# A fast matrix product on one core: the first two groups of rows in another order

## The chip, the cores and the metric

The kernel runs on one core of a Trainium2 chip. The metric is device time in microseconds (us) of one execution, the median over runs on the chip. Work is spread over engines that run side by side and wait for one another through semaphores: TensorE (PE; its weight loads are shown apart as PEld), VectorE (DVE), ScalarE (ACT), GpSimd (POOL), and SyncE (SP), which here issues nearly all DMAs. Each engine takes its own instructions strictly in the order in which they are written for it.

## The reference

```python
x: (8, 2048, 2048) float32, w: (2048, 2048) float32
cs = np.cumsum(x, axis=1)
diff = cs - (cs shifted by one row, zeros ahead)
return np.matmul(diff, w).astype(np.float32)
```

The difference of a running sum is `x` itself, so the kernel computes `x @ w`: 16384 rows by 2048 by 2048.

## The kernel before, in words

**Stages.** Rows come in tiles of 128. The first four tiles are multiplied plainly while `w` is loaded. All others, from tile `PLAIN` = 4 on, go in groups of four tiles: `g`, `g+1`, `h = g+2`, `h+1`. Each group is multiplied with Winograd's form of Strassen's scheme: `w` is cut into blocks B11, B12, B21, B22, the rows into A11, A12 (tile g or h) and A21, A22 (tile g+1 or h+1), and sums of blocks stand for some of the products: S1 to S4 of the rows' blocks (`total`), T1 to T4 of the blocks of `w` (`less`). The first group (`group_plain`, g = 4) uses one level of the scheme. From the second group on (`group`), several of the products are computed by a second, inner level with quarter blocks (`quarter`, `in_2` to `in_5`), whose sums of `w` are made in the first groups as well. `group` runs for g = 8, 12, 16 and so on; some of its order depends on whether g is `PLAIN + 4`, that is 8, the second group.

**Before a tile can be multiplied** it passes through a chain: `load` (SyncE: a DMA of half a tile, 512 KB, into a slot of `F`), `weigh` (ScalarE, L112: the sum of magnitudes of each row), `scale_of` (VectorE, L129 and L131, then GpSimd, L132: the row's scale `s` and its inverse `u`), `narrow` (ScalarE, L143: scaled to float16 in place), `turn` (SyncE, L156: a transposing DMA of each half into the tiles `x`). The slot of `F` is free for the next load when the tile is turned.

**Products** go into eight banks of PSUM, in pairs X, Y, Z, V. `product(to, a, b, first)` is sixteen matmuls: eight slices of the contraction, two banks. `keep` (ScalarE, L541) copies a bank, scaled, into an output tile; `add` (VectorE, L544) adds a bank to an output tile; `put` (SyncE, L555) sends it out. Output tiles `c` come from a list `free` of seven (`one_c`, `pair`) in turn, and a tile given out again waits for the DMA of its last output. In the first group, C11h is kept in a part of the tile `inner` (16 to 19) that is free until the sums of the inner level are made there. A bank can be overwritten only when the `keep` or `add` before it has read it.

**Order.** The function `after` ties every instruction to the one before it on its engine, so the order in which the helpers are called is the order on each engine. There is no scheduler to change it. What moves in the text moves past everything on the same engine, and on that engine only.

Of the kernel before, what the change touches and what calls it, by code (L numbers as in the profile page):

```python
# [10 lines left out]
def kernel(  # L11
# [30 lines left out]
    PLAIN = 4  # L42
# [78 lines left out]
    def scale_of(t):  # L121
        if t < END:
            m2 = sums_of.pop(t)
            m = small.tile([P, 1], f32, name="m1")
            s = scales[t] = small.tile([P, 1], f32, name="s")
            u = unit[t] = units.tile([P, 1], f32, name="u")
            after(
                "dve",
                lambda: nc.vector.tensor_scalar(m, m2[:, :1], m2[:, 1:], TINY, ADD, MAX),  # L129
            )  # L130
            after("dve", lambda: nc.vector.reciprocal(s, m))  # L131
            after("pool", lambda: nc.gpsimd.tensor_scalar(u, m, uw, None, MUL))  # L132
# [330 lines left out]
    def pair():  # L463
        return [one_c() for _ in range(2)]
# [34 lines left out]
    def less(dst, p, q):  # L499
        for k in range(len(dst)):  # L500
            after("dve", lambda: nc.vector.tensor_tensor(dst[k], p[k], q[k], SUB))  # L501

    def total(dst, p, q, op):
        after("dve", lambda: nc.vector.tensor_tensor(dst.all, p.all, q.all, op))  # L504
# [21 lines left out]
    def product(to, a, b, first):  # L526
        for some in steps(to, a, b, first, 4):
            some()
# [14 lines left out]
    def add(c, p, u):  # L543
        after("dve", lambda: nc.vector.scalar_tensor_tensor(c, p, u, c, MUL, ADD))  # L544

    def keeps(c, p, u):
        for n in range(2):
            keep(c[n], p[n], u)

    def adds(c, p, u):  # L550
        for n in range(2):
            add(c[n], p[n], u)
# [7 lines left out]
    def puts(c, t, h):  # L560
        for n in range(2):
            put(c[n], t, 2 * h + n)
# [26 lines left out]
    def group_plain(g, X, Y, Z, V):  # L589
        h = g + 2  # L590
        ug, uh, vg = unit[g], unit[h], unit[g + 1]
        A11g, A12g = parts(g)
        A11h, A12h = parts(h)
        A21g, A22g = parts(g + 1)
        A21h, A22h = parts(h + 1)
        S1g, S1h = S1
        S2g, S2h, S3g, S3h, S4g, S4h = A11g, A11h, A21g, A21h, A12g, A12h
        load(g + 4, 0)
        load(g + 4, 1)
        product(X, A11g, B11, True)  # L600
        for k in range(3):
            block(B22, 1, 1, k, "act")
        C11g = pair()
        keeps(C11g, X, ug)
        for k in range(3, KH):
            block(B22, 1, 1, k, "act" if k < 6 else "dve")
        product(V, A12g, B21, True)
        product(Y, A11h, B11, True)
        adds(C11g, V, ug)
        puts(C11g, g, 0)  # L610
        total(S1g, A21g, A22g, ADD)
        total(S3g, A11g, A21g, SUB)
        total(S2g, S1g, A11g, SUB)
        less(T2[:4], B22[:4], T1[:4])
        product(Z, A12h, B21, True)
        weigh(h + 1)
        C11h = [inner[:, ds(j, 2), :].rearrange("p a n -> p (a n)").bitcast(f32) for j in (16, 18)]
        keeps(C11h, Y, uh)
        scale_of(h + 1)
        narrow(h + 1)  # L620
        turn(h + 1)
        load(h + 4, 0)
        less(T2[4:], B22[4:], T1[4:])
        vh = unit[h + 1]
        product(V, S1g, T1, True)
        C22 = pair()
        keeps(C22, V, vg)
        total(S4g, A12g, S2g, SUB)
        product(X, S2g, T2, False)
        C12g = pair()  # L630
        keeps(C12g, X, ug)
        less(T3, B22, B12)
        product(V, S4g, B22, False)
        weigh(g + 4)
        scale_of(g + 4)
        narrow(g + 4)
        load(h + 4, 1)
        turn(g + 4)
        load(g + 5, 0)
        load(g + 5, 1)  # L640
        product(X, S3g, T3, False)
        total(S1h, A21h, A22h, ADD)
        total(S3h, A11h, A21h, SUB)
        total(S2h, S1h, A11h, SUB)
        adds(C11h, Z, uh)
        puts(C11h, h, 0)
        del free[-2:]
        adds(C12g, V, ug)
        puts(C12g, g, 1)
        product(Y, S2h, T2, False)  # L650
        C12h = pair()
        keeps(C12h, Y, uh)
        adds(C22, X, vg)
        puts(C22, g + 1, 1)
        total(S4h, A12h, S2h, SUB)
        product(Z, S1h, T1, True)
        weigh(h + 4)
        less(T4, B21, T2)
        scale_of(h + 4)
        C22 = pair()  # L660
        keeps(C22, Z, vh)
        narrow(h + 4)
        weigh(g + 5)
        product(Y, S3h, T3, False)
        in_2.first()
        in_2.fourth()
        load(h + 5, 0)
        load(h + 5, 1)
        scale_of(g + 5)
        adds(C22, Y, vh)  # L670
        puts(C22, h + 1, 1)
        product(Z, S4h, B22, False)
        in_2.third()
        adds(C12h, Z, uh)
        puts(C12h, h, 1)
        narrow(g + 5)
        turn(h + 4)
        product(X, A22g, T4, False)
        C21 = pair()
        keeps(C21, X, vg)  # L680
        puts(C21, g + 1, 0)
        turn(g + 5)
        load(g + 8, 0)
        load(g + 8, 1)
        product(Y, A22h, T4, False)
        weigh(h + 5)
        less(in_3.Q1, in_3.t12, in_3.t11)
        scale_of(h + 5)
        narrow(h + 5)
        less(in_3.Q2, in_3.t22, in_3.Q1)  # L690
        turn(h + 5)
        C21 = pair()
        keeps(C21, Y, vh)
        puts(C21, h + 1, 0)


    def group(g, X, Y, q, e, v, w):
# [56 lines left out]
        a11, a12, a22, s1, s2, s3, s4 = A2  # L754
        Q = in_2
        quarter(q, a11, Q.t11, True)
        add(C11g[0], q, ug)
        quarter(e, s1, Q.Q1, True)
        add(C11h[1], e, uh)
        if g == PLAIN + 4:  # L760
            total(S1g, A21g, A22g, ADD)
            total(S3g, A11g, A21g, SUB)
            total(S2g, S1g, A11g, SUB)
        quarter(v, a12, Q.t21, True)
        add(C11g[0], v, ug)
# [3 lines left out]
        quarter(e, s4, Q.t22, False)  # L769
        add(C11g[1], e, ug)  # L770
        put(C11g[1], g, 1)
        if g > PLAIN + 4:
            total(S1h, A21h, A22h, ADD)
            total(S3h, A11h, A21h, SUB)
        scale_of(next_g)
        narrow(next_g)
        if g > PLAIN + 4:
            total(S2h, S1h, A11h, SUB)
        go(P6g, 2)
        quarter(q, s3, Q.Q3, False)  # L780
        add(C11h[1], q, uh)
        put(C11h[1], h, 1)
        if g == PLAIN + 4:
            total(S1h, A21h, A22h, ADD)
            total(S3h, A11h, A21h, SUB)
            total(S2h, S1h, A11h, SUB)
        weigh(next_h)
        load(next_k, 1)
        total(S4g, A12g, S2g, SUB)
        go(P6g, 2)  # L790
        C12g = pair()
        keeps(C12g, X, ug)
        turn(next_g, [0])
        quarter(q, a22, Q.Q4, False)
        add(C11h[0], q, uh)
# [5 lines left out]
        if five:  # L801
            one()
            two()
        scale_of(next_h)
        narrow(next_h)
        load(next_l, 1)
        one, two, A3 = sums_in(
            S4g, S4h, (S2h.half(0), S2h.half(1), S4h.half(0), passing[2])
        )
# [86 lines left out]
        else:  # L896
            if g == PLAIN + 4:
                in_3.third()
            one()
            two()  # L900
            weigh(next_k)
            seven(A3, in_3, C12g, C12h, P7g)
            turn(next_g, [1])
# [108 lines left out]
```

## Time and profile before

| | us |
|---|---|
| median of 3 runs | 1492.88 (1492.49 to 1496.3) |
| the profiled execution | 1496.11 |
| its span, first to last instruction | 1494.3 |
| TensorE busy | 1473.4 (99%) |
| VectorE busy | 1283.9 (86%) |
| ScalarE busy | 913.6 (61%) |
| granted clock of TensorE | 0.999 |

Times within the profile are counted from the start of the span. A row of a timeline has the start, the time to the end of the last of the merged instructions, engine, line, operation, what is written and read, their number, and in brackets the idle time of the engine before it with what ended that. The first group's products begin near 76 us, the second group's near 127 us, the third's near 177 us, the fourth's near 223 us. A program line of a helper stands for all its uses: L501 is `less`, L504 `total`, L514 a matmul of `product`, L533 one of `quarter`, L555 `put`.

### The profile page before, as it was taken

The numbers are of one execution on the slowest core, as the hardware profiler recorded it, in microseconds if no ns is written. First come the engines' busy times: TensorE is split into PE (matmuls) and PEld (weight loads), VectorE is DVE, ScalarE is ACT, GpSimd is POOL, SyncE is SP. The second block draws the span as 40 slices with busy tenths as digits, with TensorE's granted clock in tenths as the row PEclk, the third lists the DMA queues.
The fourth block names the chain that finished last, engine by engine and source line by source line (L and its number), as shares of the span: only waits on it lengthen the run. The fifth ranks groups of instructions, "written<-read, shape, count | busy, mean of one in ns | idle before, by whom it ended". The sixth has DMA issues, their size and how long they took to land.

```text
span 1494.3 us, 21105 instructions
## 1 busy us (share of the span) xinstructions
PE 1473.4 (99%) x6793; PEld 663.4 (44%) x6799; DVE 1283.9 (86%) x2419; ACT 913.6 (61%) x1301; POOL 69.4 (5%) x136
## 2 busy tenths in 40 slices
PE   8999999999999999999999999999999999999998
PEld 3444444444444444444444444444444444444443
DVE  7997878888888888888888888888888888888887
ACT  5876565655666656666656656556657556656542
POOL 0110000000000000000000000000000000000000
PEclk9999999999999999999999999999999999999999
DMA  9999979999999999999999998999899999899973
GB/s 362 352 233 254 244 224 255 263 271 249 259 258 241 260 276 250 255 251 251 265 269 242 266 248 255 261 272 248 257 239 261 268 257 262 252 238 265 273 204 130
DMA packets 386255, 382.59 MB, mean 256 GB/s; under 512 B 275744, under 2 KB 275744, under 8 KB 386016
## 3 DMA queue, kind: packets, MB, share of 16 engines
q1 hardware_dynamic: 385584, 379.41, 92.6%
q0 software_dynamic: 560, 1.84, 0.3%
q8 instruction: 53, 0.87, 0.2%
q14 instruction: 58, 0.48, 0.1%
HBM read 180.88 MB, written 135.27 MB: 212 GB/s over the span
## 4 chain that ended last, share of the span: by engine, by line
PE 88%; DMA 5%; DVE 3%; ACT 2%; issue 1%; SPq 1%; DVEq 0%; ACTq 0%
PE b L533 45%; PE b L514 41%; DVE c L544 2%; PE b L250 2%; DMA W<-in_w_dram 2%; DMA F<-in_x_dram 2%; DMA x<-F 1%; DVE W L501 1%; ACT waste L112 0%; DMA W<-in_x_dram 0%; DMA out_dram<-wb 0%; ACT F L143 0%; SPq L156 0%; DVE x L504 0%; ACT wb L234 0%
## 5 line engine op out<-in xcount | busy, mean ns | idle before, releaser
L544 DVE SCALAR_TENSOR_TENSOR c<-b,u,c 128x512 f32<-128x512 f32 x1046 | 743.2, 746 | 161.6 <-PE b L533 91.5
L514 PE MATMUL b<-W,x 128*128 128x512 f16 x3072 | 717.4, 379 | 4.3 <-ACT c L541 3.5
L541 ACT ACTIVATE c<-b,u 128x512 f32<-128x512 f32 x494 | 315.9, 681 | 334.5 <-PE b L533 164.0
L514 PEld LDWEIGHTS <-x 128*128 128x128 f16 x3072 | 300.3, 98 | 369.1 <-issue 6.3
L143 ACT ACTIVATE F<-F,s 128x1024 f16<-128x1024 f32 x246 | 282.2, 1147 | 111.2 <-DVE s L131 107.2
L533 PE MATMUL b<-W,inner 128*128 128x512 f16 x1392 | 338.3, 379 | 0.0
L112 ACT ACTIVATE waste<-F 128x1024 uint8<-128x1024 f32 x246 | 259.6, 1055 | 107.5 <-DMA F<-in_x_dram 103.7
L533 PEld LDWEIGHTS <-inner 128*128 128x128 f16 x1744 | 170.6, 98 | 207.1 <-issue 1.6
L533 PEld LDWEIGHTS <-x 128*128 128x128 f16 x1560 | 152.4, 98 | 192.3 <-issue 12.2
L533 PE MATMUL b<-W,x 128*128 128x512 f16 x968 | 234.3, 379 | 1.7 <-DVE c L544 0.3
L504 DVE TENSOR_TENSOR x<-x,x 128x1024 f16<-128x1024 f16 (+1 forms) x214 | 120.5, 574 | 6.2 <-PE b L514 1.1
L132 POOL TENSOR_SCALAR u<-m,uw 128x1 f32<-128x1 f32 x124 | 64.4, 525 | 1311.3 <-DVE m L129 1303.3
L533 PE MATMUL b<-flow,x 128*128 128x512 f16 x352 | 90.3, 379 | 0.7 <-DVE c L544 0.7
L504 DVE TENSOR_TENSOR inner<-x,x 128x1024 f16<-128x1024 f16 (+1 forms) x122 | 67.5, 553 | 1.2 <-DMA x<-F 1.1
L533 PE MATMUL b<-inner 128*128 128x512 f16 x240 | 61.6, 379 | 1.1 <-DVE c L544 1.1
L250 PE MATMUL b<-wb,xP 128*128 128x512 bf16 x234 | 57.0, 393 | 5.4 <-ACT wb L234 3.8
L533 PE MATMUL b<-inner,x 128*128 128x512 f16 x240 | 61.6, 379 | 0.0
L112 ACT ACTIVATION_READ_ACCUMULATOR waste<-F 128x1 f32 x246 | 46.6, 190 | 0.0
L504 DVE TENSOR_TENSOR x<-inner,x 128x1024 f16<-128x1024 f16 x62 | 42.4, 684 | 3.2
L504 DVE TENSOR_TENSOR inner<-inner 128x512 f16<-128x512 f16 x112 | 42.4, 420 | 1.0
L501 DVE TENSOR_TENSOR flow<-W,inner 128x512 f16<-128x512 f16 x120 | 42.6, 416 | 0.0
L234 ACT CAST wb<-W 128x1024 bf16<-128x1024 f32 x32 | 32.2, 1059 | 15.6 <-DMA W<-in_w_dram 12.3
(56 smaller groups left out, 420.0 us busy)
## 6 DMA issues: line engine op xcount, KB each, us to landing
out_dram<-c SPq DMA_DIRECT2D x494, 256.0 KB, 4.1
F<-in_x_dram SPq DMA_DIRECT2D x246, 512.0 KB, 5.2
flow<-spill SPq DMA_DIRECT2D x57, 512.0 KB, 4.8
W<-in_w_dram SPq DMA_DIRECT2D x32, 512.0 KB, 10.0
W<-in_x_dram SPq DMA_DIRECT2D x16, 256.0 KB, 7.2
x<-F SPq DMA_TRANSPOSE x246, 4.0
out_dram<-o POOLq DMA_DIRECT2D x5, 256.0 KB, 4.1
out_dram<-o SPq DMA_DIRECT2D x5, 256.0 KB, 3.6
```

The source lines that it names most:

```text
L112: lambda: nc.scalar.activation(waste, where[t][i], ABS, scale=1.0 / ROW, accum_out=sums_of[t][:, i : i + 1],),
L132: after("pool", lambda: nc.gpsimd.tensor_scalar(u, m, uw, None, MUL))
L143: lambda: nc.scalar.activation(narrowed(t)[:, ds(i * NH, NH)], where[t][i], COPY, scale=s),
L234: after("act", lambda: nc.scalar.copy(b, wt))
L250: lambda: nc.tensor.matmul(ps[r][n], xP[:, r, ko, :], wb[h, ko][:, ds(n * NB, NB)], start=(ko == 0), stop=(ko == KO - 1),),
L501: after("dve", lambda: nc.vector.tensor_tensor(dst[k], p[k], q[k], SUB))
L504: after("dve", lambda: nc.vector.tensor_tensor(dst.all, p.all, q.all, op))
L514: said = nc.tensor.matmul(to[n], a[k], b[k][:, n, :], start=(first and k == 0), stop=(k == KH - 1), skip_group_check=True,)
L533: said = nc.tensor.matmul(to, a[k], b[k], start=(first and k == 0), stop=(k == 3), skip_group_check=True)
L541: after("act", lambda: nc.scalar.activation(c, p, COPY, scale=u))
L544: after("dve", lambda: nc.vector.scalar_tensor_tensor(c, p, u, c, MUL, ADD))
```

## The change

Nothing is added or left out; instructions are put in another order, and one pair of output tiles lies elsewhere.

In `group_plain` (first group):
- T2 = B22 - T1, eight pieces: the first goes ahead of `adds(C11g)`, the second behind it, four behind the sums of x, and two behind `scale_of(h + 1)` (before: four and four). T4 is split around `scale_of(h + 4)`.
- C22g lies in `inner` (20 to 23) rather than in two tiles `c`; its `keeps` go ahead of `narrow(h + 1)`. Likewise `keeps(C21, Y)` goes ahead of `narrow(h + 5)`.
- The transposes of h+4 and g+5 are issued one half at a time, some earlier; those of h+5 go ahead of the two loads of g+8. `weigh(h + 5)` is earlier.

In `group` with g = 8 (second group):
- S1g and S3g go between the additions of the first two quarter products; S1h, S3h and S2h ahead of `scale_of(next_g)` and its narrowing, which go behind half of the product P6g (X, S2g, T2) and one quarter product.
- `keeps(C12g)` goes ahead of `weigh(next_h)`; `scale_of(next_h)`, `narrow(next_h)` and one load go behind the product P6h (Y, S2h, T2), its keeps and the sums of x that `seven` needs.

Later groups keep their order.

```diff
@@ group_plain
         product(Y, A11h, B11, True)
+        less(T2[:1], B22[:1], T1[:1])
         adds(C11g, V, ug)
         puts(C11g, g, 0)
+        less(T2[1:2], B22[1:2], T1[1:2])
         total(S1g, A21g, A22g, ADD)
         total(S3g, A11g, A21g, SUB)
         total(S2g, S1g, A11g, SUB)
-        less(T2[:4], B22[:4], T1[:4])
+        less(T2[2:6], B22[2:6], T1[2:6])
         product(Z, A12h, B21, True)
         weigh(h + 1)
-        C11h = [inner[:, ds(j, 2), :].rearrange("p a n -> p (a n)").bitcast(f32) for j in (16, 18)]
+        C11h, C22g = (
+            [
+                inner[:, ds(j, 2), :].rearrange("p a n -> p (a n)").bitcast(f32)
+                for j in (i, i + 2)
+            ]
+            for i in (16, 20)
+        )
         keeps(C11h, Y, uh)
         scale_of(h + 1)
+        less(T2[6:], B22[6:], T1[6:])
+        vh = unit[h + 1]
+        product(V, S1g, T1, True)
+        keeps(C22g, V, vg)
         narrow(h + 1)
         turn(h + 1)
         load(h + 4, 0)
-        less(T2[4:], B22[4:], T1[4:])
-        vh = unit[h + 1]
-        product(V, S1g, T1, True)
-        C22 = pair()
-        keeps(C22, V, vg)
         total(S4g, A12g, S2g, SUB)
         product(X, S2g, T2, False)
         C12g = pair()
...
-        adds(C22, X, vg)
-        puts(C22, g + 1, 1)
+        adds(C22g, X, vg)
+        puts(C22g, g + 1, 1)
+        del free[-2:]
         total(S4h, A12h, S2h, SUB)
         product(Z, S1h, T1, True)
         weigh(h + 4)
-        less(T4, B21, T2)
+        less(T4[:4], B21[:4], T2[:4])
         scale_of(h + 4)
-        C22 = pair()
-        keeps(C22, Z, vh)
+        less(T4[4:], B21[4:], T2[4:])
+        C22h = pair()
+        keeps(C22h, Z, vh)
         narrow(h + 4)
         weigh(g + 5)
         product(Y, S3h, T3, False)
...
         load(h + 5, 0)
         load(h + 5, 1)
+        turn(h + 4, [0])
         scale_of(g + 5)
...
         narrow(g + 5)
-        turn(h + 4)
+        weigh(h + 5)
+        turn(h + 4, [1])
+        turn(g + 5, [0])
         product(X, A22g, T4, False)
         C21 = pair()
         keeps(C21, X, vg)
         puts(C21, g + 1, 0)
-        turn(g + 5)
-        load(g + 8, 0)
-        load(g + 8, 1)
+        turn(g + 5, [1])
         product(Y, A22h, T4, False)
-        weigh(h + 5)
         less(in_3.Q1, in_3.t12, in_3.t11)
         scale_of(h + 5)
+        C21 = pair()
+        keeps(C21, Y, vh)
         narrow(h + 5)
         less(in_3.Q2, in_3.t22, in_3.Q1)
         turn(h + 5)
-        C21 = pair()
-        keeps(C21, Y, vh)
+        load(g + 8, 0)
+        load(g + 8, 1)
         puts(C21, h + 1, 0)
@@ group
         quarter(q, a11, Q.t11, True)
+        if g == PLAIN + 4:
+            total(S1g, A21g, A22g, ADD)
         add(C11g[0], q, ug)
+        if g == PLAIN + 4:
+            total(S3g, A11g, A21g, SUB)
         quarter(e, s1, Q.Q1, True)
         add(C11h[1], e, uh)
         if g == PLAIN + 4:
-            total(S1g, A21g, A22g, ADD)
-            total(S3g, A11g, A21g, SUB)
             total(S2g, S1g, A11g, SUB)
...
         put(C11g[1], g, 1)
+        total(S1h, A21h, A22h, ADD)
+        total(S3h, A11h, A21h, SUB)
+        if g == PLAIN + 4:
+            total(S2h, S1h, A11h, SUB)
         if g > PLAIN + 4:
-            total(S1h, A21h, A22h, ADD)
-            total(S3h, A11h, A21h, SUB)
-        scale_of(next_g)
-        narrow(next_g)
-        if g > PLAIN + 4:
+            scale_of(next_g)
+            narrow(next_g)
             total(S2h, S1h, A11h, SUB)
         go(P6g, 2)
         quarter(q, s3, Q.Q3, False)
         add(C11h[1], q, uh)
         put(C11h[1], h, 1)
         if g == PLAIN + 4:
-            total(S1h, A21h, A22h, ADD)
-            total(S3h, A11h, A21h, SUB)
-            total(S2h, S1h, A11h, SUB)
-        weigh(next_h)
+            scale_of(next_g)
+            narrow(next_g)
+        else:
+            weigh(next_h)
         load(next_k, 1)
         total(S4g, A12g, S2g, SUB)
         go(P6g, 2)
         C12g = pair()
         keeps(C12g, X, ug)
+        if g == PLAIN + 4:
+            weigh(next_h)
         turn(next_g, [0])
...
-        scale_of(next_h)
-        narrow(next_h)
-        load(next_l, 1)
+        if g > PLAIN + 4:
+            scale_of(next_h)
+            narrow(next_h)
+            load(next_l, 1)
...
             one()
             two()
+            if g == PLAIN + 4:
+                scale_of(next_h)
+                narrow(next_h)
+                load(next_l, 1)
             weigh(next_k)
             seven(A3, in_3, C12g, C12h, P7g)
```

More of the change, by code (lines that the diff above doesn't have):

```diff
@@ L668, in group_plain @@
         load(h + 5, 1)
+        turn(h + 4, [0])
         scale_of(g + 5)
-        adds(C22, Y, vh)
-        puts(C22, h + 1, 1)
+        adds(C22h, Y, vh)
+        puts(C22h, h + 1, 1)
         product(Z, S4h, B22, False)
```

## The prediction

> **What bounds the kernel now.** I read the page first, then the table of stretches, then the timelines of TensorE, VectorE, ScalarE and SyncE from 85 to 159 us, where the edited code runs.
>
> ```profile
> PE 1473.4 (99%) x6793; PEld 663.4 (44%) x6799; DVE 1283.9 (86%) x2419; ACT 913.6 (61%) x1301; POOL 69.4 (5%) x136
> PE 88%; DMA 5%; DVE 3%; ACT 2%; issue 1%; SPq 1%; DVEq 0%; ACTq 0%
> ```
>
> TensorE is busy 99% of the span and is 88% of the chain that ended last. The change moves no matmul, so it can only win time in which TensorE stands still. The table of stretches (length, then busy time and count for each engine, TensorE's matmuls first and its weight loads second) says where that is:
>
> ```profile
> 85.00:159.00 74.00, 69.38 (x312) 30.12 (x310) 58.63 (x120) 51.44 (x74) 5.20 (x7) 1.00 0.94 245
> ...
> 229.00:244.00 15.00, 13.17 (x62) 5.79 (x60) 11.97 (x22) 7.39 (x11) 0.77 (x1) 1.00 1.07 288
> 244.00:1440.00 1196.00, 1194.78 (x5518) 539.58 (x5517) 1043.21 (x1993) 736.97 (x1063) 50.72 (x106) 1.00 0.95 256
> ```
>
> Each matmul has one weight load, and the loads are all recorded. From 244 to 1440 us a pair takes 1196/5517 = 0.2168 us, with nothing to win. At that pace the 310 pairs of 85 to 159 us (most of the first group and of the second) need 67.2 us of 74: 6.8 us are lost, and 2.0 more from 229 to 244 us, in the fourth group, which is not edited. 6.8 us is thus the ceiling for what the change can remove. TensorE's timeline splits it:
>
> ```profile
> 93.31 4.40 PE L514 MATMUL b<-W,x 128*128 128x512 f16 x16
> 98.15 0.38 PE L514 MATMUL b<-W,x 128*128 128x512 f16 x1 [0.44 <-ACT c L541]
> 98.73 10.30 PE L514 MATMUL b<-W,x 128*128 128x512 f16 x47 [0.20 <-ACT c L541]
> ...
> 117.33 13.76 PE L514 MATMUL b<-W,x 128*128 128x512 f16 x63 [1.18 <-ACT c L541]
> 131.48 0.38 PE L514 MATMUL b<-W,x 128*128 128x512 f16 x1 [0.40 <-ACT c L541]
> 132.06 3.40 PE L514 MATMUL b<-W,x 128*128 128x512 f16 x15 [0.20 <-ACT c L541]
> ...
> 140.18 1.90 PE L514 MATMUL b<-W,x 128*128 128x512 f16 x8 [0.40 <-DVE x L504]
> ...
> 145.84 3.63 PE L514 MATMUL b<-W,x 128*128 128x512 f16 x16 [0.31 <-DVE x L504]
> 150.33 0.38 PE L514 MATMUL b<-W,x 128*128 128x512 f16 x1 [0.86 <-ACT c L541]
> 150.91 0.81 PE L514 MATMUL b<-W,x 128*128 128x512 f16 x3 [0.20 <-ACT c L541]
> ...
> 156.38 1.02 PE L533 MATMUL b<-W,x 128*128 128x512 f16 x4 [0.29 <-DVE c L544]
> ```
>
> Sixteen matmuls without a stall take 3.63 us (the 145.84 row), one alone 0.38. A matmul so starts 0.217 after the one before but is drawn 0.38 long, and a stall costs its bracket plus 0.16. That gives: the 93.31 product, 4.40 where 3.63 is due, 0.77; 98.15 and 98.73, 0.60 + 0.36; 117.33, 1.34; 131.48 and 132.06, 0.56 + 0.36; 140.18, 0.56; 145.84, 0.47; 150.33 and 150.91, 1.02 + 0.36; 156.38, 0.45. Sum 6.85, which agrees with 6.8. It is a string of small waits with different causes, so the change goes through one by one.
>
> **The change part by part.** First group, VectorE. Its rows, with T2, T3 and the sums of x in order:
>
> ```profile
> 94.26 0.21 DVE L129 TENSOR_SCALAR m<-m 128x1 f32<-128x1 f32 x1 [2.12 <-ACT waste L112]
> ...
> 94.59 2.48 DVE L501 TENSOR_TENSOR W<-W 128x1024 f16<-128x1024 f16 x4
> ...
> 97.58 4.90 DVE L501 TENSOR_TENSOR W<-W 128x1024 f16<-128x1024 f16 x8
> 102.40 0.21 DVE L129 TENSOR_SCALAR m<-m 128x1 f32<-128x1 f32 x1
> ...
> 104.25 0.69 DVE L504 TENSOR_TENSOR x<-inner,x 128x1024 f16<-128x1024 f16 x1
> ```
>
> The scale at 94.26 waits 2.12 us for ScalarE's weighing, which waited for its load, and four pieces of T2 are queued behind it. They come every 0.60 us (2.48 for four); `product(X, S2g, T2)` uses one per 0.43 us: hence the 0.77. In the new order two pieces stand behind the scale, six ahead. The last two end at about 95.26 and 95.87; the product, begun at 93.31, wants them at 95.9 and 96.3. The 0.77 goes, with 0.5 us to spare. The two pieces now put around `adds(C11g)` cost nothing: their 1.2 us come out of the 2.12 us of idle time ahead of the scale, and S1g, 0.6 us later at most, is wanted a whole product later.
>
> ScalarE's rows for the same place, and for the later ones:
>
> ```profile
> 94.06 1.25 ACT L541 ACTIVATE inner<-b,u 128x512 f32<-128x512 f32 x2
> 95.20 2.32 ACT L143 ACTIVATE F<-F,s 128x1024 f16<-128x1024 f32 x2
> 97.43 2.40 ACT L541 ACTIVATE c<-b,u 128x512 f32<-128x512 f32 x4
> ...
> 101.86 0.19 ACT L112 ACTIVATION_READ_ACCUMULATOR waste<-F 128x1 f32 x1
> ...
> 116.59 0.69 ACT L541 ACTIVATE c<-b,u 128x512 f32<-128x512 f32 x1 [3.55 <-DMA out_dram<-c]
> ...
> 128.53 2.33 ACT L143 ACTIVATE F<-F,s 128x1024 f16<-128x1024 f32 x2 [0.55 <-DVE s L131]
> 130.76 2.40 ACT L541 ACTIVATE c<-b,u 128x512 f32<-128x512 f32 x4
> ...
> 138.17 1.06 ACT L112 ACTIVATE waste<-F 128x1024 uint8<-128x1024 f32 x1 [1.58 <-DMA F<-in_x_dram]
> ...
> 148.55 1.06 ACT L112 ACTIVATE waste<-F 128x1024 uint8<-128x1024 f32 x1 [0.35 <-DMA F<-in_x_dram]
> ...
> 149.61 1.25 ACT L541 ACTIVATE c<-b,u 128x512 f32<-128x512 f32 x2
> ```
>
> The keep of C22 that `product(V, S4g, B22)` waits for at 98.15 runs at 97.43 behind 2.32 us of narrowing. Ahead of it, it runs at 95.2 and ends by 96.5, just before V is wanted (93.31 + 3.47 = 96.8): 0.96 goes. The price is on the narrowing: two keeps (1.14 us, from 94.06 to 95.20) are now ahead of it, so its two transposes are issued 1.14 us later, and the sums S1h, S3h, S2h that end at 104.94 need both.
>
> **A new wait** comes here. In the row 98.73 x47 the product Y (S2h, T2) starts with the 32nd matmul, at 98.73 + 31 x 0.217 = 105.45, half a microsecond after S2h. Without the 0.77 + 0.96 = 1.73 us lost before, TensorE is there at 103.7. How early is S2h? T3 (97.58 row) moves up by the two pieces, 1.2 us, and frees VectorE at 101.3; but the scale at 102.40 also needs ScalarE's sums (101.86 + 0.19 = 102.05), whose time does not move, since keeps and narrowing only change places. So everything from 102.40 on comes 0.3 us earlier and S2h ends at 104.65: TensorE waits 1.0 us, where it waited not at all. If the later transposes land after 102.4, it is more: up to 1.7, all that was won. Of 1.73 us, 0.7 stays (0 to 1.1). Behind that wait nothing else is queued on TensorE's path but its own next products.
>
> The pair of C22 in the inner tile: at 116.59 the second keep of C22h waits 3.55 us for an output DMA to give back its `c`, and TensorE loses 1.34 at 117.33. With C22g in `inner`, two tiles of `c` more are free. ScalarE goes on up to 3.5 us earlier, into the next narrowing, the load that needs its slot, and the transposes. `inner` 20 to 23 are wanted again only by `in_3.Q2` at the group's end, five products of 3.47 us after C22g's output is issued; no output waits for that long here (3.55 is the worst above). 1.34 goes.
>
> At the end of the group, `keeps(C21, Y)` runs at 130.76 behind the narrowing of 128.53. Ahead of it, it runs one product before Y is wanted: 0.92 goes.
>
> Second group. VectorE's sums, and SyncE's issues of the transposes that feed them:
>
> ```profile
> 137.99 0.68 DVE L504 TENSOR_TENSOR inner<-x,x 128x1024 f16<-128x1024 f16 x1
> ...
> 139.43 0.69 DVE L504 TENSOR_TENSOR x<-inner,x 128x1024 f16<-128x1024 f16 x1
> ...
> 143.65 0.68 DVE L504 TENSOR_TENSOR inner<-x,x 128x1024 f16<-128x1024 f16 x1
> ...
> 145.09 0.69 DVE L504 TENSOR_TENSOR x<-inner,x 128x1024 f16<-128x1024 f16 x1
> ```
>
> ```profile
> 126.65 2.66 SPq L156 DMA_TRANSPOSE x<-F  x2
> ...
> 133.29 1.03 SPq L100 DMA_DIRECT2D F<-in_x_dram  x2
> 134.37 5.92 SPq L156 DMA_TRANSPOSE x<-F  x2
> ```
>
> S2g ends at 140.12 and lets TensorE go at 140.18; S2h ends at 145.78 and does so at 145.84. S1g and S3g now come between the additions ahead of 137.99, so that S2g ends at least one addition earlier: 0.56 goes. The price is on those additions: VectorE takes its work in order, and a late transpose of g+5 would hold an addition and with it the bank that TensorE's next quarter product writes; the transposes of g+5 had landed when S1g began at 137.99, and ScalarE's part of them now comes earlier. S2h moves ahead of the scale and of the addition at 142.98, but what it can win depends on SyncE: its transposes (134.37) took 5.92 us to issue, where a pair usually takes 2.66, with two loads just ahead. The issue of the second ended at 140.3, and S1h, which needs both, began at 143.65. In the new order the two loads and the puts of C21h are queued on SyncE behind these transposes, and the transposes of h+4 and g+5 are issued one by one, each as its narrowing ends; ScalarE's narrowing itself is up to 3.5 us earlier. I take it that all land early enough: 0.47 goes. (The gain cannot be over 0.47; what it costs if not is rival 1.)
>
> [...]
>
> `keeps(C12g)` goes ahead of `weigh(next_h)`, whose second half (148.55) waits for its load and holds the keep until 149.61: 1.38 goes. The scale of next_h is taken out of the row of additions behind which TensorE waits at 156.38: 0.45 or a part of it.
>
> Sum: 6.85 off, 1.0 on: 5.85. Three waits on VectorE (0.56, 0.47, 0.45; 1.5 together) have the thinnest margins, and I leave a third of them: **5.4 us**. The profiled execution took 1496.11 us (span 1494.3) and would take 1490.7. It is 3.2 us above the median of 1492.88, and I cannot see where these lie. Taking the 5.4 as whole, the median comes to **1487.5**. If the 3.2 are stalls of this stretch that the median run does not have, only 2.2 is left: 1490.7.
>
> **Rivals.** (1) The transposes land no earlier. If S1h still starts at 143.65, S2h lets TensorE go at 145.84 again, while TensorE would be at that product at 145.84 - 0.47 - 0.56 - 0.92 - 1.34 - 0.73 = 141.8. It waits 4.0 us: 1491.5, within 0.3%. For it speaks the 5.92 us row, against it that the loads are out of its way. With the case of the 3.2 us above (1490.7) it makes up what I give to no change.
>
> (2) Slower: the loads, held back. The two of 133.29 feed the weighing at 138.17, which already waits 1.58 us for its half. Issued only behind both transposes, at worst at 140.3, they land some 7 us later, and so does each narrowing that frees a slot of `F` for the next load. The fourth group loses 2.0 us (229 to 244 us) as it is. If the lateness is handed on, every later group pays. It is slower from the point at which the 27 groups behind 244 us lose 0.37 us each (5.4 + 4.5 = 9.9 us); at 12 us in all it ends at 1487.5 + 12 = 1499.5. Against it: 1196 us without a loss, with the same order of transfers, so that a lateness is made good there.
>
> The built order has the instructions where the text puts them, and TensorE's unchanged, so that nothing is done is no rival.
>
> **How the numbers follow.** 0.3% of the median, about what a measurement of this kernel can tell from no change, is 4.5 us: faster below 1488.4. The forecast has 0.68: each of its removals has a row with its cause, and the 5.4 may be 1 us less and still count. Rival 1 and its like have 0.24, rival 2 0.08. The range reaches from 1484.5 (all 6.85, only 0.3 of the new wait, and 1.9 of the 2.0 us at 229 us) to 1492.0 (0.9 won), so that both cases of no change are in it and rival 2 is left out.
>
> **What would show it.** In the new profile the brackets at 98, 117, 131 and 150 us are gone; one of about 0.8 (1.0 lost) by VectorE's L504 stands near 104 us; the keep of C22h has no wait for an output DMA; the weight loads from 85 to 159 us number some 335, not 310. A bracket over 2 us in the second group behind L504 would be rival 1; brackets on L533 or L514 in each group behind 244 us, rival 2. The forecast is wrong if the lost time from 85 to 159 us stays above 3 us.

## The result, and the profile after

The changed kernel takes 1490.65 us (median of 7 runs, 1489.3 to 1491.43), the kernel before, run beside it on the same chip, 1495.11 (7 runs, 1492.49 to 1497.16): a ratio of 0.997, 95% interval 0.9959 to 0.9982. That is 4.5 us less (2.7 to 6.1 by the interval). The forecast time was 1487.5, with a range of 1484.5 to 1492.0. The gain, 4.46 us, is just short of the 4.5 us (0.3%) from which the prediction called it faster, and the time stays above the 1488.4 that it named.

The profiled execution of the changed kernel took 1489.75 us, its span is 1488.0. The page and the table of stretches, in the columns shown before:

```profile
PE 1471.8 (99%) x6793; PEld 663.9 (45%) x6799; DVE 1284.0 (86%) x2419; ACT 914.1 (61%) x1301; POOL 69.9 (5%) x136
PE 92%; DMA 3%; DVE 2%; ACT 2%; issue 1%; SPq 0%; DVEq 0%; ACTq 0%
...
85.00:159.00 74.00, 73.05 (x338) 32.85 (x337) 63.44 (x135) 53.83 (x77) 6.50 (x8) 1.00 0.92 245
```

From 85 to 159 us 337 weight loads stand where 310 stood: 27 x 0.2168 = 5.9 us, and 74 - 337 x 0.2168 = 0.9 us are still lost of 6.8. TensorE's timeline has one stall left in the two edited groups, and two in the fourth group, which is not edited:

```profile
92.34 10.52 PE L514 MATMUL b<-W,x 128*128 128x512 f16 x48
103.81 3.41 PE L514 MATMUL b<-W,x 128*128 128x512 f16 x15 [0.95 <-DVE x L504]
...
227.92 1.02 PE L533 MATMUL b<-inner 128*128 128x512 f16 x4 [1.17 <-DVE c L544]
235.01 1.02 PE L533 MATMUL b<-flow,x 128*128 128x512 f16 x4 [0.88 <-DVE c L544]
```

The stall at 103.81 is the new wait of the forecast. It is seen from VectorE's side and from ScalarE's:

```profile
93.70 1.27 DVE L501 TENSOR_TENSOR W<-W 128x1024 f16<-128x1024 f16 x2
...
95.49 4.90 DVE L501 TENSOR_TENSOR W<-W 128x1024 f16<-128x1024 f16 x8
101.20 0.21 DVE L129 TENSOR_SCALAR m<-m 128x1 f32<-128x1 f32 x1 [0.81 <-ACT waste L112]
...
103.06 0.69 DVE L504 TENSOR_TENSOR x<-inner,x 128x1024 f16<-128x1024 f16 x1
```

```profile
90.77 1.06 ACT L112 ACTIVATE waste<-F 128x1024 uint8<-128x1024 f32 x1 [2.01 <-DMA F<-in_x_dram]
...
92.11 1.06 ACT L112 ACTIVATE waste<-F 128x1024 uint8<-128x1024 f32 x1 [0.20 <-DMA F<-in_x_dram]
...
95.45 2.35 ACT L143 ACTIVATE F<-F,s 128x1024 f16<-128x1024 f32 x2
...
110.77 1.27 ACT L541 ACTIVATE c<-b,u 128x512 f32<-128x512 f32 x2
111.93 2.33 ACT L143 ACTIVATE F<-F,s 128x1024 f16<-128x1024 f32 x2
```

VectorE is through with T3 and then waits 0.81 us for ScalarE's sums, as foretold; S2h ends at 103.75 and TensorE goes on at 103.81. The keeps of C22h (110.77) wait for no output DMA, and the narrowing behind them starts at 111.93 instead of 117.18.

### The profile page after: what moved, and what is told of

It reads as the page before. It is cut to its first block, busy times and chain, and to the rows that moved or that the text cites. A ratio compares the mean times of both kernels' runs of the same rounds, so it can differ in the third digit from the quotient of the medians.

```text
span 1488.0 us, 21103 instructions
## 1 busy us (share of the span) xinstructions
PE 1471.8 (99%) x6793; PEld 663.9 (45%) x6799; DVE 1284.0 (86%) x2419; ACT 914.1 (61%) x1301; POOL 69.9 (5%) x136
## 4 chain that ended last, share of the span: by engine, by line
PE 92%; DMA 3%; DVE 2%; ACT 2%; issue 1%; SPq 0%; DVEq 0%; ACTq 0%
PE b L533 46%; PE b L514 43%; PE b L250 2%; DVE c L544 2%; DMA W<-in_w_dram 1%; DMA x<-F 1%; DMA F<-in_x_dram 0%; ACT wb L234 0%; DMA out_dram<-wb 0%; ACT waste L112 0%; ACT o L270 0%; DVE inner L504 0%; ACT F L143 0%; ACT xP L220 0%; DVE x L504 0%
## 5 line engine op out<-in xcount | busy, mean ns | idle before, releaser
L237 DVE TENSOR_REDUCE wmax<-W 128x1 f32<-128x1024 f32 x32 | 39.0, 1220 | 3.3 <-DMA W<-in_w_dram 1.7
```

The source lines that it names most:

```text
L237: lambda: nc.vector.tensor_reduce(wmax[:, i : i + 1], wt, AX.X, MAX, apply_absolute_value=True),
```

## The experiments

Times are medians; ratios are to the kernel before on the same chip. The last two columns are counted from each kernel's one trace: weight loads of TensorE in the two edited groups (some 341 would be no loss) and in the third and fourth (159 to 244 us, 392).

| kernel | us | ratio (95%) | loads 85-159 | loads 159-244 |
|---|---|---|---|---|
| before (first trace) | | | 310 | 381 |
| before (second trace) | 1495.82, one run | | 314 | 377 |
| changed | 1490.65 | 0.997 (0.9959-0.9982) | 337 | 380 |
| first group's edits alone | 1490.7 | 0.9973 (0.9963-0.9983) | 337 | 376 |
| second group's edits alone | 1493.91 | 0.9995 (0.9986-1.0005) | 325 | 382 |
| changed, pair back in `c` | 1491.74 | 0.9978 (0.9969-0.9987) | 328 | 381 |
| before, pair in `inner` alone | 1492.63 | 0.999 (0.9981-0.9999) | 322 | 381 |
| changed, narrowing first | 1490.87 | 0.9973 (0.9962-0.9984) | 342 | 378 |
| changed, T2 four and four | 1490.38 | 0.9969 (0.9957-0.998) | 336 | 377 |
| changed, loads ahead of transposes | 1490.32 | 0.9967 (0.9955-0.9978) | 334 | 383 |
| changed, h+1 loaded early | 1489.6 | 0.9964 (0.9951-0.9978) | 339 | 382 |
| before, h+1 loaded early | 1494.87 | 0.9999 (0.999-1.0008) | 309 | 382 |
| changed, fourth group's transpose | 1488.25 | 0.9956 (0.9939-0.9972) | 337 | 389 |
| changed, early load and transpose | 1487.79 | 0.9954 (0.994-0.9967) | 339 | 391 |

An edit worth under 1 us is not resolved by the medians (the intervals are some 3 to 5 us wide); for those the traces are compared. Two cautions go with that. Each changed kernel has one trace, and in two of them (the first group's edits alone, the narrowing first) the loads of h+1 landed early without an edit that would explain it, and the stall near 104 us (1.1 us, five loads) is not there. And what one stretch wins the next can lose again, so the sum of the two columns counts: 691 in both traces of the kernel before, 717 in the changed kernel.

**Which group brings it.** The first run has the diff of `group_plain` only, the second that of `group` only.

> The edits of group_plain alone; the second group is as before. Lost time is counted as the length of 85 to 159 us less 0.2168 us for each weight load in it (before 6.8 us, with the whole change 0.9). Theory (each wait has a cause of its own, as the prediction has it): the brackets at 98, 117 and 131 us go, one of 0.95 us stands near 104 us, and those of the second group stay (S2g 0.56, C12g's keep 1.38, the additions 0.45): about 3.5 us lost, 3.3 won against before. Rival (the second group's waits are really set by when its loads and transposes arrive, and these come from the first group): with the first group's order alone they go too, and under 2 us is lost.

> The edits of the second group alone; group_plain is as before. Theory: the first group's 1.73 + 1.34 + 0.92 us stay, C12g's keep (1.38) and most of the additions (0.45) and of S2g (0.56) go, and S2h (0.47) stays, since its transposes still go behind two loads: 4.4 to 4.9 us lost from 85 to 159 us, about 2 won against before. Rival (transposes set it all): the sums of x wait for them wherever they stand, 5.5 us or more lost.

In the median the first group's edits alone give the whole: 1490.7 us. Their 337 loads owe something to the early landing (ScalarE; the changed kernel weighs at 90.77 and 92.11):

```profile
89.10 1.05 ACT L112 ACTIVATE waste<-F 128x1024 uint8<-128x1024 f32 x1
...
90.99 1.06 ACT L112 ACTIVATE waste<-F 128x1024 uint8<-128x1024 f32 x1 [0.75 <-DMA F<-in_x_dram]
```

They are thus better compared with the 342 of the other trace with an early landing, which has the second group's edits too. Of the four stalls that the second group had in the kernel before, TensorE's timeline of the run without them keeps two,

```profile
135.66 1.90 PE L514 MATMUL b<-W,x 128*128 128x512 f16 x8 [0.41 <-DVE x L504]
141.32 4.49 PE L514 MATMUL b<-W,x 128*128 128x512 f16 x20 [0.31 <-DVE x L504]
```

those of S2g and S2h, unchanged in length, 1.0 us together with what a stall costs beside its bracket. That is what the second group's edits win in the stretch beside the first group's; the medians (1490.7 and 1490.65) do not show it. The keeps of C12g (1.38) and the last additions (0.45) hold nothing up any more, though the second group's own order is the old one: with an earlier first group that order costs nothing here. The second group's edits alone show no change in the median. In their trace the stalls at 140, 145, 150 and 156 us are gone as well, but a new one stands there, and it says what they lack (timelines of TensorE, VectorE and SyncE):

```profile
143.83 1.02 PE L533 MATMUL b<-flow,x 128*128 128x512 f16 x4 [1.73 <-DVE c L544]
```

```profile
140.97 0.69 DVE L504 TENSOR_TENSOR inner<-x,x 128x1024 f16<-128x1024 f16 x1 [1.75 <-DMA x<-F]
```

```profile
132.42 5.91 SPq L156 DMA_TRANSPOSE x<-F  x2
```

With the first group's order on SyncE as before, the transposes again take 5.91 us to issue. S1h, now ahead of an addition, waits 1.75 us for them and holds that addition, and TensorE with it. (3.5 us are lost, not the 4.4 to 4.9 expected, but that is luck: this execution took 1493.04 us, under its median, and has no stall of 1.34 at the keep of C22h, which waits 2.17 us for its output DMA and not 3.55.)

**The pair of C22g.** Once taken out of the changed kernel, once put alone into the kernel before:

```diff
-        C11h, C22g = (... inner[:, ds(j, 2), :] ... for i in (16, 20))
+        C11h = [inner[:, ds(j, 2), :]... for j in (16, 18)]
+        C22g = pair()
...
         puts(C22g, g + 1, 1)
-        del free[-2:]
```

> The whole change, but C22g lies in two tiles c of the list again. Theory: the second keep of C22h waits for an output DMA of a tile c as before (3.55 us there), TensorE loses 0.8 to 1.4 us near 116 us, and 1.7 to 2.4 us are lost from 85 to 159 us. Rival (with the keeps ahead of the narrowings the tile is back in time): no bracket near 116 us, 0.9 us lost.

> The kernel before with one edit: the pair of the first group's C22g lies in the inner tile (20 to 23) in place of two tiles c. Order untouched. Theory (handed on): the second keep of C22h no longer waits 3.5 us for an output DMA, so the narrowing behind it (117.18 us before, 111.93 in the changed kernel) comes some 4 us earlier, and with it the loads and transposes behind it. Then 1.34 at 117 goes, and with it 1.38 at 150 and 0.45 at 156, which hang on a load that lands late; 93, 98 and 131 us (0.77, 0.96, 0.92) stay, for they come from the order of ScalarE and VectorE and from the load of h+1. 140 and 145 (0.56, 0.47) are open: gone if the transposes' lateness alone sets them. 322 to 329 weight loads in 85 to 159 us in place of 310 to 314, 2.5 to 4 us faster than before. Rival (each stall its own cause, as the sum of the prediction lists them): only 1.34 goes: 316 to 320 loads, 1.3 us faster or less.

With the pair back in `c`, 2.9 us are lost, where 1.7 to 2.4 were expected; ScalarE and TensorE stand as in the kernel before, or worse:

```profile
116.23 0.69 ACT L541 ACTIVATE c<-b,u 128x512 f32<-128x512 f32 x1 [4.12 <-DMA out_dram<-c]
```

```profile
116.97 10.52 PE L514 MATMUL b<-W,x 128*128 128x512 f16 x48 [1.75 <-ACT c L541]
```

Alone, it brings 12 loads (2.6 us in the trace, 2.0 in the median, by the interval 0.1 to 2.8). TensorE's timeline of that run from the end of the first group on:

```profile
129.32 3.40 PE L514 MATMUL b<-W,x 128*128 128x512 f16 x15 [0.20 <-ACT c L541]
...
137.44 1.90 PE L514 MATMUL b<-W,x 128*128 128x512 f16 x8 [0.40 <-DVE x L504]
143.10 3.91 PE L514 MATMUL b<-W,x 128*128 128x512 f16 x17 [0.31 <-DVE x L504]
147.21 0.81 PE L514 MATMUL b<-W,x 128*128 128x512 f16 x3 [0.20 <-ACT c L541]
152.69 1.02 PE L533 MATMUL b<-W,x 128*128 128x512 f16 x4 [0.29 <-DVE c L544]
```

The stall at 117 us is gone, and with it 0.56 of the 0.92 at 131 us and 1.02 of the 1.38 of C12g's keeps, all by this one edit. S2g and S2h stay to the hundredth, and no trace with the second group's edits has them, so their cause is the second group's order. The last additions' 0.45 stays too: the expectation had it go, and what in the first group's other edits removes it was not tried.

**The first stalls, at 93 and 98 us.** Two runs undo one edit each in the changed kernel: `narrow(h + 1)` ahead of `keeps(C22g, V)` again, and T2 cut four and four again.

```diff
+        narrow(h + 1)
         product(V, S1g, T1, True)
         keeps(C22g, V, vg)
-        narrow(h + 1)
```

> The changed kernel, but narrow(h+1) stands ahead of keeps(C22g, V) again. Theory (a floor): S2h is set by ScalarE's weigh of h+1 and the scale behind it, which end at about 102 us whatever stands behind the narrowing, so Y(S2h, T2) starts near 104.8 us with or without the 0.96 us that the swap saves at 98 us. The stall of 0.4 to 1.0 us at 98 us comes back and the one near 104 us shrinks by as much, or a little less: 0 to 0.3 us of TensorE's time lost against the changed kernel, 337 weight loads or one less in 85 to 159 us, and a time within 0.5 us of 1490.7. Rival (each edit wins its own stall, as the sum of the prediction first lists it): the narrowing gains 1.14 us with its transposes, S2h comes earlier, but 0.96 us come back in full at 98 us: 333 loads, about 1 us slower. Third case: the narrowing behind the keeps is what makes S2h late, so that without the swap the stall near 104 us goes altogether: 1 us lost at 98, 1 us won at 104, and the start of Y(S2h, T2) comes earlier than 103.5 us.

```diff
-        less(T2[2:6], B22[2:6], T1[2:6])
+        less(T2[:4], B22[:4], T1[:4])
...
-        less(T2[6:], B22[6:], T1[6:])
+        less(T2[4:], B22[4:], T1[4:])
```

> The changed kernel, but T2's pieces stand four ahead of the scale of g+4 and four behind it, as in the kernel before, in place of six and two. Theory (a floor): the product of 93 us is slowed again by up to 0.8 us (its 16 matmuls take up to 4.4 us in place of 3.63), but Y(S2h, T2) waits for S2h near 104 us all the same, or 0.3 us longer as T3 comes later by two pieces; the stall at 104 us gives back what the product lost. 0 to 0.3 us lost in all, 336 to 337 loads in 85 to 159 us, a time within 0.5 us of 1490.7. Rival (each edit wins its own stall): 0.77 us lost and not given back, 333 to 334 loads, 0.8 us slower. Where the weighing of h+1 happens to end early, the scale waits for nothing and neither stall shows.

T2 cut as before: the floor holds. The product slows, and the wait shrinks by what it lost (TensorE):

```profile
92.32 11.49 PE L514 MATMUL b<-W,x 128*128 128x512 f16 x48
104.02 3.19 PE L514 MATMUL b<-W,x 128*128 128x512 f16 x14 [0.20 <-DVE x L504]
```

48 matmuls take 11.49 instead of 10.52, and the bracket is 0.20 instead of 0.95; the product Y starts at 104.02 against 103.81. The narrowing first showed neither stall, at 98 or at 104, which no theory had said. The cause is not the edit, whose instructions run after 91 us, but something earlier in that execution (ScalarE, VectorE, TensorE):

```profile
88.87 1.06 ACT L112 ACTIVATE waste<-F 128x1024 uint8<-128x1024 f32 x1
...
90.11 1.06 ACT L112 ACTIVATE waste<-F 128x1024 uint8<-128x1024 f32 x1
```

```profile
101.36 0.69 DVE L504 TENSOR_TENSOR x<-inner,x 128x1024 f16<-128x1024 f16 x1
```

```profile
92.55 13.98 PE L514 MATMUL b<-W,x 128*128 128x512 f16 x64
```

The loads of h+1 had landed some 2 us earlier than in the changed kernel's trace, so the weighing waited for nothing. S2h starts 11.25 us behind the second weighing here (90.11 to 101.36), 10.95 in the changed kernel (92.11 to 103.06), 10.93 with the first group alone (90.99 to 101.92, and no stall either) and 11.25 before (93.00 to 104.25). In these traces S2h keeps its distance to the landing of that load, whatever stands between. Narrowing first thus does not bring S2h forward, as the third case had it; what that order costs at 98 us when the landing is late, this trace cannot show. The distance became the next theory, and two runs move nothing but the two loads, in the changed kernel and in the kernel before:

```diff
+        load(PLAIN + 3, 0)
+        load(PLAIN + 3, 1)
         for c, rows, columns in done:
             after("sp", lambda: put(c, rows, columns, nc.sync))
...
         left_over(bank(2))
-        load(PLAIN + 3, 0)
-        load(PLAIN + 3, 1)
```

> The changed kernel, but the two loads of the first h+1 (line 421) are issued ahead of the row of output DMAs of the setup, some 9 us earlier on SyncE; nothing else moves. Theory (one cause): S2h of the first group ends 11.0 to 11.3 us after the second of these loads lands (92.03 us and 103.06 in the changed kernel's trace, 90.03 and 101.36 in the experiment with the narrowing first), so with the landing before 86 us the weighing starts at 88.8 as soon as ScalarE is free, S2h is there by 102 us and the wait of 1.1 us near 104 us is gone: 340 to 342 weight loads in 85 to 159 us, about 1 us faster than 1490.7. Rival: the DMA engines are full from 75 to 85 us, and 1 MB put ahead makes the transposes of g+1 (issued at 81 us) and S1g late by up to 2.6 us: a new wait ahead of the product of 92 us, as long as the one removed or longer, 1490.7 or more.

> The kernel before with nothing but the two loads of the first h+1 issued ahead of the row of output DMAs of the setup; no edit of either group. Theory (one cause): the stalls at 93 and 98 us come from the landing of these loads at 92 to 93 us, which holds the scale on VectorE, and the keeps on ScalarE behind the narrowing. With an earlier landing the scale waits for nothing, the keep of C22 ends two microseconds earlier, and both go without any edit of the order: 1.7 us. Those that follow from the first group's lateness (1.38 at 150, 0.45 at 156) may go too; 117, 131, 140 and 145 stay (3.3 us): 318 to 326 weight loads in 85 to 159 us in place of 310 to 314, 1.7 to 3.6 us faster than before. Rival (order, as the prediction has it): the pieces behind the scale and the keep behind the narrowing cost what they cost, since the narrowing still comes ahead of the keep: 0.96 at 98 stays and only 0.77 at 93 goes; 314 to 318 loads, under 1 us faster.

In the changed kernel the wait near 104 us goes. S2h starts at 101.90; the two loads, issued at 74.54, landed within 7.1 us and nothing waited for them, so with a landing this early it is no longer the landing alone that sets it. Over half of what that wins is paid by the rival's mechanism, transposes of g+1 that land late (VectorE, then TensorE):

```profile
88.64 0.69 DVE L504 TENSOR_TENSOR inner<-x,x 128x1024 f16<-128x1024 f16 x1 [1.50 <-DMA x<-xP]
```

```profile
89.54 3.61 PE L514 MATMUL b<-W,inner 128*128 128x512 f16 x16 [0.45 <-PE b L514]
```

1489.6 us: the medians do not part it from 1490.65. In the kernel before, no stall is left at 93 or at 98 us, though not an instruction of the two groups was moved: the theory of one cause is right there. But its forecast of 1.7 to 3.6 us is wrong; nothing is won. What comes behind takes it all back (TensorE):

```profile
116.31 13.76 PE L514 MATMUL b<-W,x 128*128 128x512 f16 x63 [1.65 <-ACT c L541]
...
149.87 0.38 PE L514 MATMUL b<-W,x 128*128 128x512 f16 x1 [1.44 <-ACT c L541]
150.45 0.81 PE L514 MATMUL b<-W,x 128*128 128x512 f16 x3 [0.20 <-ACT c L541]
```

1.65 where 1.15 to 1.18 stood, 1.44 where 0.61 to 0.86 stood, and a new 0.46 at 89.6. At these two places TensorE goes on only 1.0 and 0.5 us earlier than in the first trace (116.31 for 117.33, 149.87 for 150.33). The keep that it waits for at the first starts at 115.57 for 116.59. In the two traces of the kernel before, that keep waits 3.55 and 3.52 us for an output DMA and starts 6.76 and 6.72 us behind the issue of the outputs ahead of it (109.83 and 108.95); here it waits 4.02 us, and the profile names VectorE as its releaser. That a tile `c` comes back no sooner here either is the author's estimate; what holds the second keep was not shown. While such waits stood behind it, being early was worth nothing.

**The loads of g+8.**

```diff
+        load(g + 8, 0)
+        load(g + 8, 1)
         scale_of(h + 5)
...
         turn(h + 5)
-        load(g + 8, 0)
-        load(g + 8, 1)
```

> The changed kernel, but the two loads of group g+8 are issued ahead of the scale, narrowing and transposes of h+5 again, as in the kernel before; the transposes are still issued one by one. The prediction's step: the loads on SyncE ahead of the transposes made these late (5.92 us to issue), so S2h of the second group is late again and TensorE loses 0.47 us or more behind VectorE's L504 near 141 us, up to the 4 us of its first rival if the transposes are issued as late as in the kernel before. Rival: the earlier narrowing (the pair of C22g in the inner tile, keeps ahead) is what brought S2h forward, the loads' place is worth nothing: transposes land 1 to 2 us later, still ahead of VectorE's sums, 0 to 0.2 us lost, 336 to 338 loads in 85 to 159 us, a time within 0.5 us of 1490.7.

SyncE, VectorE and TensorE of that run:

```profile
128.74 1.05 SPq L100 DMA_DIRECT2D F<-in_x_dram  x2
129.89 4.96 SPq L156 DMA_TRANSPOSE x<-F  x2
```

```profile
139.09 0.69 DVE L504 TENSOR_TENSOR inner<-x,x 128x1024 f16<-128x1024 f16 x1 [0.58 <-DMA x<-F]
```

```profile
141.94 1.02 PE L533 MATMUL b<-flow,x 128*128 128x512 f16 x4 [0.56 <-DVE c L544]
```

S1h waits for its transposes again, and TensorE loses 0.56 + 0.16. So the place of the loads is worth some 0.7 us in this stretch, as the prediction's step had it. In the whole it does not show: the fourth group has one stall in that trace instead of two (as a consequence or by chance, no run shows), the loads up to 244 us add up to the same 717 (334 + 383, 337 + 380), and the medians, 1490.32 and 1490.65, are alike. In the changed kernel three transposes issue in 4.23 us ahead of the loads, and S1h waits for nothing.

**The kernel before again.**

> The kernel before once more, for a second trace of it. If the stalls of 85 to 159 us are set by the order of the work, all eight come again within 0.2 us each, 6.8 us lost in all. If those of the second group (140, 145, 150, 156 us) and the one at 117 us follow from how late loads and output DMAs happen to land, they differ from the first trace by half a microsecond or more, while those at 93, 98 and 131 us, which come from ScalarE's and VectorE's order alone, stay.

The bracketed stalls at 98, 117, 131, 140, 145 and 156 us come again with 0.44 and 0.20, 1.15, 0.40 and 0.20, 0.41, 0.31, and 0.29. Two differ, the one that is handed on at 150 us (0.61 for 0.86) and, against the expectation, that of the product at 93 us:

```profile
92.95 3.86 PE L514 MATMUL b<-W,x 128*128 128x512 f16 x16
```

Its 16 matmuls take 3.86 us, not 4.40: the second weighing of h+1 began at 92.10, not at 93.00, and the pieces of T2 behind the scale came as much earlier. 314 loads: against this trace the change wins 23 x 0.2168 = 5.0 us in the stretch, against the first 5.9.

**The fourth group.** In the group with g = 12, `turn(next_h, [1])` is called right behind `turn(next_h, [0])`; then the same with the early load of h+1.

```diff
             turn(next_h, [0])
+            if g == PLAIN + 8:
+                turn(next_h, [1])
...
         keep(C21g[0], q, vg)
-        turn(next_h, [1])
+        if g != PLAIN + 8:
+            turn(next_h, [1])
```

> The whole change, and in the third group (g = 12) the second half of h+4's tile is turned right behind its first half, not two products later. The stalls that are left after the change are two in the fourth group (1.17 and 0.88 us idle, 2.4 us lost with what a stall costs beside its bracket). Theory: they come from transposes issued last in the third group, one at a time behind a full queue; one taken out of that tail brings them 1 us earlier or more, and 1 to 2 us of the 2.4 go. Rival (the tail is bound by the transfers themselves, not by their order): both brackets stay within 0.3 us.

> The changed kernel with the two loads of the first h+1 ahead of the setup's output DMAs, and with the second transpose of next_h in the third group issued right behind the first, as in the experiment on the fourth group. Theory: the two are at different places and add up: no wait of TensorE over 0.2 us from 85 to 244 us, 342 weight loads in 85 to 159 us, 1 us off the 1488.25 of the fourth group's experiment: 1487.2. Rival: the earlier first group only moves the fourth group's lateness: its sums wait for loads whose time is set by SyncE's queue and not by TensorE, so that what is won near 104 us is lost again at 228 us: 1488.2.

SyncE and VectorE, in the changed kernel and then in the first of these runs:

```profile
216.04 1.43 SPq L156 DMA_TRANSPOSE x<-F  x1
...
218.19 5.48 SPq L156 DMA_TRANSPOSE x<-F  x2
...
223.53 0.42 DVE L504 TENSOR_TENSOR inner<-x 128x512 f16<-128x512 f16 x1 [1.71 <-DMA x<-F]
```

```profile
194.67 5.83 SPq L156 DMA_TRANSPOSE x<-F  x3
...
216.91 4.72 SPq L156 DMA_TRANSPOSE x<-F  x2
...
222.05 0.42 DVE L504 TENSOR_TENSOR inner<-x 128x512 f16<-128x512 f16 x1
```

One transpose less is queued ahead of the pair that VectorE waits for; both stalls of the fourth group are under 0.2 us (the first is 0.99 or more in each of the twelve traces without this edit), and the loads from 159 to 244 us rise from 380 to 389. The expectation of 1 to 2 us is met or passed (2.4 in the median). At 1488.25 us each of the four runs (1486.86 to 1488.73) is below each of the changed kernel's seven, though these were not run beside them. With the early load as well it is 1487.79 us (5 runs, 1486.58 to 1488.84; 0.9954, 0.994 to 0.9967), the fastest measured. Its TensorE has no stall over 0.2 us from 91 to 250 us; one is left ahead of that, so that 339 loads stand where 342 were expected:

```profile
89.22 3.61 PE L514 MATMUL b<-W,inner 128*128 128x512 f16 x16 [0.36 <-PE b L514]
```

The span (1484.8, against 1486.4 and 1487.6 for each alone) looks as if the two added up, but this trace is of the fastest of the five runs. By the medians the last 0.5 us are not certain, and the rival's 1488.2 is no farther off than the theory's 1487.2.

## Why the prediction was right or wrong

**The gain, right.** Net of the new wait it foretold 5.85 us for the stretch, and 5.4 with the discount; the traces show 5.9 and 5.0, the median 4.5 with 5.4 inside its interval. The discount (a third of the three VectorE waits) was not needed in that trace: none of the three is left.

**The new wait, right.** Foretold: a bracket of 0.8 (1.0 lost) near 104 us, because the scale of g+4 needs ScalarE's sums, which do not move. Measured: 0.95 (1.11 lost), behind those sums. So of the first 1.73 us 0.6 stays (0.7 foretold), and the T2 edit is worth 0.2 us. The wait hangs on a late landing of h+1's loads, which the prediction took from the one trace that it had: two traces with an early one do not have it.

**117, 140 and 145 us, right, each by its own edit or order:** 1.34 goes by the pair and comes back as 1.91 without it; two traces without the second group's edits have 0.56 and 0.47 as before, and none with them has either. The 0.92 at 131 us is gone too, but the swap of keep and narrowing, to which the prediction gave all of it, is not its only remedy: 0.56 goes with the pair alone. The price named for the sums ahead of an addition, a late transpose that holds a bank, is what the second group's edits alone paid (1.73 bracket) and what the loads' old place pays (0.56). Rival 1 names the same lateness; it is real, but in these traces it costs 0.7 to 1.9 us and not 4.0, and the new order on SyncE is part of what keeps it off.

**150 and 156 us, right in size, one step short in cause.** The step said that `keeps(C12g)` behind `weigh(next_h)` costs 1.38, and the scale among the additions 0.45. Both go with the first group's edits alone, in the old order, and both are absent with the second group's edits alone. The keep is late where the weighing ahead of it waits for its load (until 148.55 in the trace before); with the first group's edits alone that weighing (140.74 and 141.90) waits for nothing, and the second group's edits put the keep ahead of it. Of the 0.45 it stays open which part of the first group's edits removes it. A sum that books each stall in full to the edit next to it gives some edits too much: the last four terms come to 2.9 us, and the second group's edits are worth 1.0 us in the stretch beside the first group's, and no measurable time alone.

**93 and 98 us: the row was read one step too short.** The scale waits and the keep stands behind the narrowing, but both wait only because h+1's load lands at 92 us; with that load early the old order stalls at neither. The edits do what was forecast where the landing is late: the changed kernel weighs at 92.11 and has neither stall, the second trace of the kernel before weighs at 92.10 and has both, the first in part.

**The transposes.** In landing they were no slower than the outputs, 3.7 us against 4.8 in the issue table of the changed kernel from 100 to 140 us (KB each, median us from issue to landing; half a tile in float16 is 256 KB; the outputs go to DRAM and the transposes do not, so the two are not quite alike):

```profile
out_dram<-c SPq DMA_DIRECT2D x12, 256.0 KB, 4.8
...
x<-F SPq DMA_TRANSPOSE x8, 3.7
```

On the issuing engine they took longer (SyncE, the same kernel):

```profile
122.35 2.67 SPq L156 DMA_TRANSPOSE x<-F  x2
125.11 1.02 SPq L555 DMA_DIRECT2D out_dram<-c  x2
126.22 4.23 SPq L156 DMA_TRANSPOSE x<-F  x3
```

The pair at 122.35 takes 2.67 us of SyncE, the two outputs behind it 1.02. The 0.47 of S2h is gone, as forecast: no trace with the second group's edits has it. What the place of the loads alone decides, 0.7 us, is made up by 244 us in the trace that shows it.

**The level, wrong by 3.15 us.** The prediction took 5.4 off 1492.88, the median of three runs. Seven runs beside the changed kernel give 1495.11, and the other sessions 1494.6 to 1495.3: 2.2 us of the miss are that median, 0.9 the gain. The profiled 1496.11, held to be 3.2 us too long, was 1.0 above the median; 1496.11 - 5.4 = 1490.7, the sum against the profiled execution's own time, would have been the better forecast. That the prediction's other case, in which the 3.2 us lie in this stretch, also gave 1490.7 is luck: it rested on a gain of 2.2.

## What to carry to other kernels

A string of small waits is not a sum of small causes: follow each back past the order next to it to the load, output or transpose that sets it, and ask which of the later ones it hands its lateness to. An early start can be taken up by a later wait: the same early loads won nothing in the kernel before (1494.87 us against 1495.28). Count the stretch behind the edit too, for the next group can give back what this one won, and compare traces in which the same loads land alike. And take the level from more than three runs, when single ones spread over 6 us.

## What the runs showed of the hardware that was not expected

The same two loads, issued at 84.10 us in one execution and 84.46 in another, let the weighing start at 88.87 without a wait, and at 90.77 after a wait of 2.01. Which of the two it is goes with no edit (issued at 84.31 us they gave 89.10, at 84.42 us 90.74), and why it is one or the other stays open; it is what a stall of 1 us near 104 us hangs on.
